# Rotary embedding on one core: empty instruction slots ahead of VectorE's and GpSimd's work

## The chip, the cores and the metric

One Trainium2 chip, of which the kernel uses one core. The metric is the device time of one execution in microseconds (us), as the median of several runs. The engines are named as in the profile: PE (TensorE matmul), PEld (its weight loads), DVE (VectorE), ACT (ScalarE), POOL (GpSimd) and SP (SyncE, which here only issues transfers). "SPq" and "ACTq" are the sequencers of SP and ACT, which start DMAs. The core has 16 DMA engines. q1 is the queue of the transfers that SP starts, q10 that of ACT, and q14, labelled "instruction" in the profile, carries program code.

## The reference

```python
# x (8, 2048, 8, 64) f32; cos, sin (2048, 32) f32
x1 = x[..., :32]
x2 = x[..., 32:]
out1 = x1 * cos - x2 * sin      # cos, sin broadcast over batch and heads
out2 = x1 * sin + x2 * cos
return concatenate([out1, out2], axis=-1)
```

The input and the output have 33.55 MB each, so the core has to move 67 MB and do about three elementwise operations on every element.

## The kernel before

Each of the 8 batch entries `b` is one tile `xt` of 128 partitions by 8192 float32 (4 MB). Five such tiles exist (`NBUF = 5`), and the result is written over the input, in place, before it is stored. SP loads the first five entries at once (`load`, L67), the first of them in pieces of 1, 1 and 2 MB with the `cos` table between; ACT's queue loads the `sin` table (L76). After each of the first three entries has been stored, the load of entry `b + 5` is issued into the buffer that came free.

An entry is worked on in units of 2048 elements for each partition (`UNIT`), or 1024 at the very beginning and end. `rotate` does one unit in one of three ways. Kind A, nearly all of them: POOL writes `t2` with two multiplications (L122, by `sin_sb` and by `nsin`, the negated table), DVE multiplies by the cosine into `t1` (L129) and adds `t1` and `t2` back into `xt` (L136). Kind B, in three units, leaves the addition to PE, which adds with an identity matrix in PSUM (L143, L144), and ACT copies the sum back (L145). Kind C, in two units, takes POOL's work away as well: DVE does a second multiplication (L148), and PE and ACT the rest (L160 to L165).

Program order is fixed on every engine by `keep`, so no scheduler moves anything. Ahead of the loop stand POOL's memset and select that build the identity `eye` (L80, L81), ACT's negated tables and DVE's copy of the cosine table into PSUM (L93). The stores of entries 0 to 6 go out on ACT's queue (L74), those of the last entry, in pieces of 2, 1 and 1 MB, on SP's queue (L74). At the end SP waits for every store (L219).

DVE's whole program is about 110 instructions, the waits on semaphores included, and POOL's about 95.

Of the kernel before, what the change touches and what calls it, by code (L numbers as in the profile page):

```python
# [10 lines left out]
def kernel(  # L11
# [7 lines left out]
    nc = tc.nc  # L19
    keep = tc.keep_in_program_order  # L20
# [43 lines left out]
    def load(b):  # L64
        xt = xpool.tile([P, ROW], f32, tag="xt", name=f"xt{b}")
        for lo, n in spans([UNIT, UNIT, 2 * UNIT] if b == 0 else [ROW]):
            keep(nc.sync.dma_start(out=xt[:, lo : lo + n], in_=xv[b, :, lo : lo + n]))  # L67
            if b == 0 and lo == 0:
                keep(nc.sync.dma_start(out=cos_sb, in_=cos_src))
        xts[b] = xt  # L70
# [6 lines left out]
    for b in range(NBUF):  # L77
        load(b)

    keep(nc.gpsimd.memset(eye, 0.0))  # L80
    nc.gpsimd.affine_select(  # L81
        out=eye,
# [141 lines left out]
```

## Time and profile before

| what | value |
|---|---|
| median of 3 runs | 163.35 us (163.29 to 163.39) |
| profiled execution, its own time | 163.35 us |
| its span, first to last instruction | 161.5 us |
| DVE busy | 140.1 us (87%) |
| POOL busy | 138.9 us (86%) |
| PE busy; ACT busy | 49.2 us; 12.8 us |
| moved by DMA over the span | 67.65 MB, mean 419 GB/s |
| share of the 16 DMA engines, q1 and q10 | 55.3% and 42.8% |

The profiled execution's own time equals the median; it is 1.85 us more than its span, and that part lies outside the instructions shown. All durations below come from this one execution. Busy time of an engine is not by itself a bound: which wait ends last decides.

### The profile page before, as it was taken

What the parts mean: (1) busy time and instruction counts of PE and PEld (TensorE: products, weight loads), DVE (VectorE), ACT (ScalarE), POOL (GpSimd) and SP (SyncE); (2) the same over time, 40 slices, a digit from 0 to 9 for tenths busy, and PEclk for the clock granted to TensorE, in tenths of its full rate; (3) what the DMA queues carried; (4) which work ended last, traced back from release to release, by engine and by line L of the source; (5) the groups of instructions that cost most, each with busy time, mean ns of one, the idle gap of its engine ahead of it and who ended that gap; (6) DMA issues with size and microseconds to landing.
All of it is one profiled execution on the core that took longest, in us unless ns stands there. A gap on an engine that the chain in (4) does not pass through costs nothing.

```text
span 161.5 us, 460 instructions
## 1 busy us (share of the span) xinstructions
PE 49.2 (30%) x80; PEld 18.5 (11%) x80; DVE 140.1 (87%) x66; ACT 12.8 (8%) x14; POOL 138.9 (86%) x70
## 2 busy tenths in 40 slices
PE   0000000597309770978039723973000000000000
PEld 0000000142004220323023302320000000000000
DVE  0297999999999999999999999999999999999600
ACT  3300000002200220021100220022000000000000
POOL 1399997999999999999994999999999999996000
PEclk9999999999975998589956995599655555555555
DMA  5999998998999999999999999999999999999994
GB/s 153 423 458 418 430 487 381 430 487 381 487 398 446 389 462 389 462 446 389 487 422 389 487 416 389 487 422 398 473 422 406 471 422 406 471 422 406 426 404 209
DMA packets 3458, 67.65 MB, mean 419 GB/s; under 512 B 384, under 2 KB 384, under 8 KB 640
## 3 DMA queue, kind: packets, MB, share of 16 engines
q1 hardware_dynamic: 2016, 38.01, 55.3%
q10 hardware_dynamic: 1440, 29.62, 42.8%
q14 instruction: 2, 0.02, 0.0%
HBM read 34.08 MB, written 33.55 MB: 419 GB/s over the span
## 4 chain that ended last, share of the span: by engine, by line
DVE 75%; POOL 9%; issue 6%; DMA 4%; DVEq 0%
DVE t L129 40%; DVE xt L136 33%; POOL t L122 9%; DMA sin_sb<-in_sin_dram 4%; DVE t L148 3%; DVEq L136 0%
## 5 line engine op out<-in xcount | busy, mean ns | idle before, releaser
L122 POOL TENSOR_TENSOR t<-xt,sin_sb 128x1024 f32<-128x1024 f32 (+1 forms) x32 | 71.2, 2226 | 8.5 <-DMA sin_sb<-in_sin_dram 5.3
L129 DVE TENSOR_TENSOR t<-xt,cos_ps 128x2048 f32<-128x2048 f32 (+1 forms) x34 | 73.4, 2166 | 0.8
L122 POOL TENSOR_TENSOR t<-xt,nsin 128x1024 f32<-128x1024 f32 (+1 forms) x32 | 71.3, 2228 | 0.0
L136 DVE TENSOR_TENSOR xt<-t,t 128x2048 f32<-128x2048 f32 (+1 forms) x29 | 62.2, 2145 | 4.2 <-POOL t L122 1.2
L143 PE MATMUL o<-t,eye 128*128 128x512 f32 x24 | 16.9, 797 | 23.1 <-DVE t L129 19.7
L160 PE MATMUL o<-t,eye 128*128 128x512 f32 x16 | 12.0, 842 | 37.9 <-DVE t L129 35.7
L144 PE MATMUL o<-t,eye 128*128 128x512 f32 x24 | 14.9, 709 | 0.0
L145 ACT COPY xt<-o 128x1024 f32<-128x1024 f32 x6 | 6.1, 1012 | 45.7 <-PE o L144 45.7
L143 PEld LDWEIGHTS o<-t,eye 128*128 128x128 f32 x24 | 5.5, 256 | 32.5 <-issue 26.6
L160 PEld LDWEIGHTS o<-t,eye 128*128 128x128 f32 x16 | 3.7, 256 | 43.4 <-issue 39.5
L165 ACT COPY xt<-o 128x1024 f32<-128x1024 f32 x4 | 4.0, 1012 | 47.8 <-PE o L161 47.8
L93 DVE COPY cos_ps<-cos_sb 128x512 f32<-128x512 f32 x1 | 0.7, 695 | 7.1 <-DMA cos_sb<-in_cos_dram 7.1
L144 PEld LDWEIGHTS o<-t,eye 128*128 128x128 f32 x24 | 5.6, 235 | 8.1 <-issue 8.1
L161 PE MATMUL o<-t,neye 128*128 128x512 f32 x8 | 6.2, 872 | 0.2
L148 DVE TENSOR_TENSOR t<-xt,sin_ps 128x2048 f32<-128x2048 f32 x2 | 4.6, 2280 | 0.0
L161 PE MATMUL o<-t,eye 128*128 128x512 f32 x8 | 4.1, 592 | 0.0
L161 PEld LDWEIGHTS o<-t,neye 128*128 128x128 f32 x8 | 2.1, 296 | 5.2 <-issue 3.6
L161 PEld LDWEIGHTS o<-t,eye 128*128 128x128 f32 x8 | 1.5, 190 | 1.9 <-issue 1.9
L90 ACT ACT_TABLE_LOAD x1 | 1.3, 1283 | 1.2 <-PEq L208 1.2
L90 ACT ACTIVATE nsin<-sin_sb 128x512 f32<-128x512 f32 x1 | 0.6, 630 | 4.1 <-DMA sin_sb<-in_sin_dram 4.1
L91 ACT COPY sin_ps<-sin_sb 128x512 f32<-128x512 f32 x1 | 0.6, 578 | 0.0
L80 POOL MEMSET eye<- 128x128 f32 x1 | 0.2, 204 | 0.3 <-POOLq L208 0.3
(6 smaller groups left out, 1.0 us busy)
## 6 DMA issues: line engine op xcount, KB each, us to landing
xt<-in_x_dram SPq DMA_DIRECT2D x7, 4096.0 KB, 34.5
out_dram<-xt ACTq DMA_DIRECT2D x6, 4096.0 KB, 30.5
xt<-in_x_dram SPq DMA_DIRECT2D x2, 1024.0 KB, 6.8
xt<-in_x_dram SPq DMA_DIRECT2D x1, 2048.0 KB, 12.3
out_dram<-xt ACTq DMA_DIRECT2D x2, 1024.0 KB, 19.3
out_dram<-xt ACTq DMA_DIRECT2D x1, 2048.0 KB, 28.0
out_dram<-xt SPq DMA_DIRECT2D x1, 2048.0 KB, 13.5
out_dram<-xt SPq DMA_DIRECT2D x2, 1024.0 KB, 9.9
```

The source lines that it names most:

```text
L90: keep(nc.scalar.mul(nsin, sin_sb, -1.0))
L93: keep(nc.vector.tensor_copy(cos_ps, cos_sb))
L122: nc.gpsimd.tensor_mul(out=t2u[:, :, u, :].rearrange("p (r h) d -> p r h d", h=H), in0=xu[:, :, 1 - u, :].rearrange("p (r h) d -> p r h d" ...
L129: nc.vector.tensor_mul(out=t1.rearrange("p (r k d) -> p r k d", r=nr, d=Dh), in0=xk, in1=rep(cos_ps[:, r0 : r0 + nr, :], 2 * H),)
L136: keep(nc.vector.tensor_add(out=xt, in0=t1, in1=t2))
L143: nc.tensor.matmul(oc, eye, t1[:, cs], start=True, stop=False)
L144: nc.tensor.matmul(oc, eye, t2[:, cs], start=False, stop=True)
L145: keep(nc.scalar.copy(xt[:, 2 * j * C : 2 * (j + 1) * C], o))
L148: nc.vector.tensor_mul(out=t2.rearrange("p (r k d) -> p r k d", r=nr, d=Dh), in0=xk, in1=rep(sin_ps[:, r0 : r0 + nr, :], 2 * H),)
L160: nc.tensor.matmul(oc, eye, t1u[:, gs, u, :], start=True, stop=False)
L161: nc.tensor.matmul(oc, eye if u else neye, t2u[:, gs, 1 - u, :], start=False, stop=True)
L165: nc.scalar.copy(xu[:, :, u, :], o.rearrange("p (g d) -> p g d", d=Dh))
```

## The change

Two directives are put behind the issue of the first loads and ahead of the first instruction of work on POOL and on DVE. A directive becomes no instruction itself. When the program is loaded, it is replaced by as many empty instructions as are needed for the next instruction of that engine to stand at the wanted place: for DVE at a multiple of 128 instruction slots, for POOL at 120 slots past a multiple of 128. How many these are, depends on how many slots the loaded program has ahead of that point, which the source doesn't tell; at most 127 each. No other instruction is added, removed or moved: on every engine the order of the rest is as before. All lines behind the directives have numbers higher by 2.

```diff
     for b in range(NBUF):
         load(b)
 
+    keep(nc.vector.addr_align(128))
+    keep(nc.gpsimd.addr_align(128, offset=120))
     keep(nc.gpsimd.memset(eye, 0.0))
     nc.gpsimd.affine_select(
```

DVE's next instruction is the copy of the cosine table (L93 before), POOL's the memset of `eye` (L80 before).

## The prediction
> **What bounds the kernel now.** I read the page's busy times first, then the DMA queues, then a table by stretches, and last the records of single DMA packets.
>
> ```profile
> PE 49.2 (30%) x80; PEld 18.5 (11%) x80; DVE 140.1 (87%) x66; ACT 12.8 (8%) x14; POOL 138.9 (86%) x70
> ...
> q1 hardware_dynamic: 2016, 38.01, 55.3%
> q10 hardware_dynamic: 1440, 29.62, 42.8%
> q14 instruction: 2, 0.02, 0.0%
> ```
>
> The two data queues take 55.3 + 42.8 = 98.1% of the 16 DMA engines' span; DVE and POOL are less full. In the table by stretches the last two columns are DMA share and GB/s:
>
> ```profile
> 1.70:3.20 1.50, 0.00 (x0) 0.00 (x0) 0.00 (x0) 0.75 (x1) 0.00 (x0) 1.00 0.94 213
> 3.20:8.00 4.80, 0.00 (x0) 0.00 (x0) 0.91 (x2) 1.35 (x3) 1.35 (x2) 1.00 1.00 406
> 8.00:94.00 86.00, 39.50 (x64) 14.72 (x64) 83.16 (x39) 7.21 (x8) 82.96 (x38) 0.88 1.01 432
> ...
> 118.00:152.00 34.00, 0.00 (x0) 0.00 (x0) 32.80 (x17) 0.00 (x0) 30.02 (x16) 0.50 1.00 431
> 152.00:159.40 7.40, 0.00 (x0) 0.00 (x0) 0.20 (x1) 0.00 (x0) 0.00 (x0) 0.50 1.00 423
> 159.40:160.40 1.00, 0.00 (x0) 0.00 (x0) 0.00 (x0) 0.00 (x0) 0.00 (x0) 0.50 0.12 49
> ```
>
> From 3.2 to 159.4 us the DMA engines are full. Before 3.2 they ramp up, and in the last microsecond only 12% of them work. DVE's last instruction starts at 150.98 and ends at 152.21; the rest is stores, for which SP waits at L219:
>
> ```profile
> SPq L219 <- DMA out_dram<-xt: 7.9, 4, 2.4
> ```
>
> So the end is set by the DMA engine that is through with its share last. Every transfer is split evenly over the 16 engines, and each engine's part of a transfer ends in a 4-byte completion record, whose ends I list. For entry 2's store (issued at 62.66) they lie at 93.98 to 94.30, a spread of 0.32. For the last store 14 lie at 159.42 to 159.74, but one at 160.03 and one at 160.36. Two engines have fallen behind, 0.62 us in all at the end. The packets that start in the last moments show it: 5 packets, of which 3 are completion records and 2 are data.
>
> ```profile
> DMA packets 5, 0.02 MB, mean 24 GB/s; under 512 B 3, under 2 KB 3, under 8 KB 3
> ```
>
> What delayed them is on the third queue. Its two packets in the span, of 8192 bytes and 309 ns each, start at 94.09 and 115.84 us; here are the DMA views of 94.0 to 94.4 and of 115.8 to 116.2 (packets, MB, share):
>
> ```profile
> q14 instruction: 1, 0.01, 4.8%
> q10 hardware_dynamic: 13, 0.00, 1.8%
> ```
> ```profile
> q1 hardware_dynamic: 11, 0.36, 212.0%
> q14 instruction: 1, 0.01, 4.8%
> ```
>
> The 32 KB data packet directly behind the first fetch took 1745 ns and that behind the second 1434, where such packets take 1213 nearly everywhere. Each engine's loss is the fetch and the stretch, less the 3 ns by which packets overlap: 309 + 532 - 3 = 838 ns and 309 + 221 - 3 = 527 ns. The first straggler appears among the completions of the next load (109.45, the others by 108.82), the second after 115.84. No engine idles after 3.1 us, so what an engine loses it never makes up. That is the one thing in this kernel that code placement can touch.
>
> **The change, part by part.**
>
> *Empty instructions on DVE.* At most 127. The trace has none; bounds for one are 21 ns (the length of DVE's semaphore records) and 69 ns (two such in a row, 116.110 to 116.179). DVE is past the opening barrier at 0.69 us, so it is ready at 0.69 to 9.5 us. Its first work waits until 7.06 for the cosine table:
>
> ```profile
> 7.06 0.69 DVE L93 COPY cos_ps<-cos_sb 128x512 f32<-128x512 f32 x1 [7.06 <-DMA cos_sb<-in_cos_dram]
> ```
>
> With a middling 64 at 34 ns (GpSimd's rate between memsets at 0.237, 0.271 and 0.305) the pad ends at 2.9 and costs nothing. The worst end is 2.4 us late.
>
> *Empty instructions on POOL.* By the same count, 0 to 127, at 34 to 79 ns (its two semaphore instructions at 0.533 and 0.612): ready at 0.7 to 10.7, middling 2.9. Its first multiplication waits until 6.64 for the sine table, and `eye` ahead of it needs 0.6 us and is first read at 7.65. Middling cost nothing, worst end 4 us late.
>
> *Who covers a late DVE or POOL.* SP and ACT issue the first loads unpadded. The later loads have over 12 us to spare: the last is issued at 94.80, and its queue is busy with the load before until 108.50. Entry 6's store is issued at 132.78, while entry 5's occupies the queue until 139.97. The last store is issued at 152.23; from issue to first packet the first load took 1.0 us, so its packets could go at 153.2, but the engines are busy with the store before it until 156.97. A shift of all DVE work by up to 3.7 us therefore adds nothing. Without that cover a late DVE would cost what it is late.
>
> *The two fetches.* The packets have 8192 bytes, which over 128 slots is 64 bytes a slot. I take one as DVE's and one as POOL's, requested when each moves into its next block of 128 slots. Both DVE and POOL issue something at 92.6, 1.5 us ahead of the first, and at about 113.8, 2.0 us ahead of the second. DVE has some 112 instructions left at the directive, POOL some 85; placed as the change wants them, each stays within one block behind the crossing. The crossings move to DVE's pad and to POOL's ninth instruction, one of its first multiplications. With 1.5 to 2.0 us of delay DVE's fetch lands at about 4.4 to 5 us, and POOL's at 8 to 10. So the fetches are not saved; they come among the first loads.
>
> What is a fetch worth there? Bounds: nothing, if it falls before about 3.1 us, when 8 KB packets take 450 to 1000 ns instead of 309 and the ramp, not the engine, is the limit; and 838 ns, as at 94 us. In between: the packet's own 309 and a stretch of the next. The stretches of 221 and 532 fell on packets of 32 KB; up to 8 us the packets have 2, 8 or 16 KB. If the stretch goes with size, at 8 KB it is a quarter, 55 to 133 ns. I take 0.36 to 0.44 us of loss per engine, nearest to the packet's own row. The two stragglers without their fetches would be at 160.36 - 0.84 = 159.52 and 160.03 - 0.53 = 159.50, where the crowd is; with the early loss they end at 159.86 to 159.96. The last completion moves from 160.36 to about 159.93, and the time by -0.4: 163.35 - 0.4 = 162.95. The floor is the crowd's own last, 159.74, that is -0.62 or 162.73.
>
> [...]
>
> **The rivals.**
>
> *The loss travels along undiminished.* If a fetch costs its engine 0.5 to 0.84 wherever it comes, the stragglers end as late as now: 163.35, at most ±0.2 with the host's place in the crowd. For: the engines are full from 3.2 us on, and the stretch may belong to the fetch and not to the packet behind. Against: the stretches already differ by 2.4 times.
>
> [...]
>
> *Both fetches on one DMA engine.* Now they sit on two. Asked for within a few microseconds of each other, they might be served by one: 0.84 + 0.53 = 1.37 behind the crowd, 159.50 + 1.37 = 160.87, half a microsecond later than now: 163.85. It turns slower once the joint loss passes 0.86. Against: the two stragglers of now. The same sign comes from a pad at its upper end on POOL, 4 us late against 3.7 of cover: +0.3.
>
> **How the numbers follow.** About 0.2%, 0.33 us, is what a measurement of this kernel can tell from no change. Early and cheaper fetches: 0.48, nearly all of it beyond -0.33 (-0.35 to -0.62). Undiminished loss, blocks elsewhere or a loss only a little smaller: 0.38, within ±0.33. One engine for both, or a pad that isn't covered: 0.14. The range reaches from the floor 162.73 (rounded down to 162.7 for the spread of runs, 0.1) to 163.6, which takes in the undiminished case and half of the slower one. The forecast's own range is 162.7 to 163.05.
>
> **What the profile would show.** Right: the two q14 packets start before about 10 us and none later; completions of the last store all within about 0.5 us, the last before 160.0; DVE's copy and POOL's first multiplication still at about 7.0 and 6.6. Wrong: a q14 packet after 20 us; a straggler beyond 160.2 in spite of early fetches; a first copy later than 7.5 with the end later too.

## The result, and the profile after

The changed kernel takes 163.61 us (median of 22 runs, 163.5 to 164.2), the kernel before 163.39 on the same chip (22 runs, 163.26 to 163.78). The ratio is 1.0016, with a 95% interval of 1.0009 to 1.0022: 0.22 us slower, which is inside the 0.2% taken as no change, but not zero by the interval. The forecast was 162.95, its range 162.7 to 163.6. The profiled execution after took 163.58 us with a span of 161.8 (161.775, before 161.548). So 1.80 us lie outside the span in both kernels (the 1.85 given for the kernel before came from its rounded span), and the whole difference, 0.23, is in the span.

Busy times and queues of the page after:

```profile
PE 49.5 (31%) x80; PEld 18.7 (12%) x80; DVE 140.1 (87%) x66; ACT 12.8 (8%) x14; POOL 138.9 (86%) x70
...
q1 hardware_dynamic: 2016, 38.01, 55.4%
q10 hardware_dynamic: 1440, 29.62, 42.6%
q14 instruction: 2, 0.02, 0.0%
```

Work and transfers are the same, down to the packet, and there are still two code packets. The records show the pads themselves: 61 empty instructions on DVE, one every 47 ns from 0.763 to 3.575 us, and 52 on POOL, one every 40 ns from 0.695 to 2.735. The first work behind them, by the timeline after (start, duration, instruction, and in brackets what it waited for):

```profile
6.40 1.27 POOL L124 TENSOR_TENSOR t<-xt,sin_sb 128x512 f32<-128x512 f32 x1 [3.01 <-DMA sin_sb<-in_sin_dram]
6.78 0.69 DVE L95 COPY cos_ps<-cos_sb 128x512 f32<-128x512 f32 x1 [6.78 <-DMA cos_sb<-in_cos_dram]
```

Both still wait for their tables and are 0.24 and 0.28 us earlier than before, so the pads are covered. The table by stretches (DMA share and GB/s in the last two columns) is as full as before:

```profile
1.70:3.20 1.50, 0.00 (x0) 0.00 (x0) 0.00 (x0) 0.75 (x1) 0.31 (x2) 1.00 0.92 225
3.20:8.00 4.80, 0.00 (x0) 0.00 (x0) 1.18 (x2) 1.35 (x3) 1.79 (x3) 1.00 1.04 426
8.00:94.00 86.00, 39.74 (x64) 14.88 (x64) 83.12 (x39) 7.39 (x8) 82.95 (x38) 0.88 1.01 430
...
152.00:159.40 7.40, 0.00 (x0) 0.00 (x0) 0.28 (x1) 0.00 (x0) 0.00 (x0) 0.50 0.99 422
159.40:160.40 1.00, 0.00 (x0) 0.00 (x0) 0.00 (x0) 0.00 (x0) 0.00 (x0) 0.50 0.14 57
```

The code packets have moved. They start at 7.48 and 10.48 us; the DMA views of 7.3 to 7.8 and of 10.3 to 10.8 each hold one (packets, MB, share):

```profile
q1 hardware_dynamic: 26, 0.21, 108.1%
q14 instruction: 1, 0.01, 3.9%
...
q1 hardware_dynamic: 15, 0.25, 118.4%
q14 instruction: 1, 0.01, 3.9%
```

The 8 KB data packet behind the first took 922 ns, 613 more than the 309 of its kind; the 16 KB packet behind the second took 921, 310 more than its kind. With the prediction's formula that is 309 + 613 - 3 = 919 and 309 + 310 - 3 = 616 ns of loss, against 838 and 527 of the late fetches before. Of the last store's 16 completion records 14 end at 159.46 to 159.77 (the crowd), one at 160.14 and one at 160.60 (the stragglers; before, 160.03 and 160.36). SP waits for them as before, and the DMA view of 159.72 to 160.7 shows three completion records and three data packets:

```profile
SPq L221 <- DMA out_dram<-xt: 8.1, 4, 2.4
```
```profile
DMA packets 6, 0.02 MB, mean 25 GB/s; under 512 B 3, under 2 KB 3, under 8 KB 3
```

**Where the 0.23 us come from.** The records do not name the DMA engine. But of the packets behind 3.2 us each starts 3 or 4 ns before the end of another (all 3401 before, 3396 of 3398 after), which is taken as the one ahead of it on its engine. With the transfers of a queue taken in the order of their issue, the engine that ends last can so be followed packet by packet from the end of its part of the cosine table. A packet's duration beyond that of its kind is called a stretch.

| the last DMA engine | before | after | difference |
|---|---|---|---|
| through with the cosine table | 6.555 | 6.258 | -0.30 |
| sum of stretches | 0.80 | 1.33 | +0.53 |
| the fetch itself | 0.306 | 0.306 | 0 |
| last completion | 160.365 | 160.605 | +0.24 |

Before, its stretches were 253 ns at 49.65 us and the 532 behind the fetch. After, they are 613 behind the fetch, 232 at 24.85, 91 at 42.07, and then 113, 109 and 116 at 71.83, 91.30 and 110.78. The other engines have stretches too (a mean of 0.36 us before and 0.66 after, most of it at about 49.5 and 40.5 us), but after 60 us they have 0.02 in the kernel after, where this engine has 0.34. Its three late ones have one place: it alone is still finishing a load on q1 that the others have done, and the packet stretched is q10's first behind that. Net of all this it lags no further: it is 0.95 us behind the median engine at the end of the load behind the fetch (9.64 us) and 0.96 behind at its last completion.

### The profile page after: what moved, and what is told of

The parts are those of the page before. It is cut to its first block, busy times and chain, and to the rows that moved or that the text cites. A ratio compares the mean times of both kernels' runs of the same rounds, so it can differ in the third digit from the quotient of the medians.

```text
span 161.8 us, 573 instructions
## 1 busy us (share of the span) xinstructions
PE 49.5 (31%) x80; PEld 18.7 (12%) x80; DVE 140.1 (87%) x66; ACT 12.8 (8%) x14; POOL 138.9 (86%) x70
## 4 chain that ended last, share of the span: by engine, by line
DMA 46%; DVE 37%; POOL 9%; issue 2%; DVEq 0%; SPq 0%; POOLq 0%; ACTq 0%
DMA xt<-in_x_dram 22%; DMA out_dram<-xt 20%; DVE t L131 18%; DVE xt L138 17%; POOL t L124 9%; DMA sin_sb<-in_sin_dram 3%; DVE t L150 1%; DVEq L138 0%; SPq L67 0%; POOLq L124 0%; ACTq L74 0%
## 5 line engine op out<-in xcount | busy, mean ns | idle before, releaser
L124 POOL TENSOR_TENSOR t<-xt,sin_sb 128x1024 f32<-128x1024 f32 (+1 forms) x32 | 70.4, 2200 | 7.7 <-DMA xt<-in_x_dram 3.3
L124 POOL TENSOR_TENSOR t<-xt,nsin 128x1024 f32<-128x1024 f32 (+1 forms) x32 | 70.4, 2200 | 0.0
L93 ACT COPY sin_ps<-sin_sb 128x512 f32<-128x512 f32 x1 | 0.6, 579 | 0.0
```

The lines of the kernel that those rows point to most:

```text
L124: nc.gpsimd.tensor_mul(out=t2u[:, :, u, :].rearrange("p (r h) d -> p r h d", h=H), in0=xu[:, :, 1 - u, :].rearrange("p (r h) d -> p r h d" ...
```

## The experiments

The times of before differ slightly between chips, so each kernel stands against runs of before on its own chip: 163.37 us for the first four kernels (30 runs), 163.45 for the next three (17), 163.43 for the last two (17). The theories were: a fetch costs its engine 0.5 to 0.9 us whenever it comes, and that decides the end; or the fetch's moment is the price; or something else (the pads, the order of work) is.

**One directive alone.** `e1_dve_only`:

```diff
+    keep(nc.vector.addr_align(128))
```

> Only DVE's directive is kept. Straggler theory: the last DMA engine is the one that carries DVE's code fetch, and GpSimd's fetch sits on another engine that is never last. Then this is as slow as the changed kernel: 163.6, ratio 1.001 to 1.002; one code packet at about 7.5 us with a stretch of some 0.6 us behind it, the other still at about 116 us with 0.2. Rival, the pads or GpSimd's late start cost the time: about half the change, 163.5, or nothing, 163.4, if it is GpSimd's pad alone.

163.71 us (11 runs, 163.5 to 164.55), ratio 1.0023 (1.0013 to 1.0034). Code packets at 7.21 us (+600 ns on the packet behind) and 115.90 (+221). Last completions: 13 at 159.39 to 159.64, then 159.87, 160.08 on the engine of the second fetch and 160.74 on that of the first. The latter has lone stretches of 51, 118 and 138 ns at 71.99, 91.41 and 110.89.

`e2_pool_only`:

```diff
+    keep(nc.gpsimd.addr_align(128, offset=120))
```

> Only GpSimd's directive is kept. Straggler theory: no difference from the kernel before, 163.4, ratio 0.9995 to 1.0005; code packets at about 10.5 us (GpSimd's) and about 94 us (DVE's), the last completion of the last store at 160.3 to 160.4. Rival, GpSimd's pad or its early fetch costs the time: 163.6.

163.45 us (11 runs, 163.32 to 163.84), ratio 1.0007 (0.9999 to 1.0016). Code packets at 10.03 (+331) and 94.08 (+532). The engine of DVE's late fetch ends at 160.355, that of POOL's early one at 160.39, after lone stretches of 203, 120, 148 and 155 ns at 24.65, 71.53, 91.01 and 110.52.

So the packet at 94 us was DVE's and that at 116 POOL's, which the prediction had left open, and each directive moves its own. DVE's accounts for the loss. POOL's early fetch ends where DVE's late one does, and its price is hidden behind that or at the edge of what can be measured.

**A program without a crossing, and the same with an early one.** `e3_short` leaves out the rotation of entries 4 to 7:

```diff
-            rotate(b, lo, n)
+            if b < 4:
+                rotate(b, lo, n)
```

> The kernel before with the rotation of entries 4 to 7 left out (they are loaded and stored as they are), so that DVE's program ends before its crossing at slot 64 of the kernel and GpSimd's before its own. The transfers are the same. Straggler theory: no code packet in the span, all 16 completions of the last store within 0.4 us, and about 0.6 us less than before if the DMA engines stay full: 162.7 to 162.9. Rival, the end is set by something other than the stragglers (arbitration of the two queues, the last store's issue): 163.3 or any other figure, with a spread of the last completions like now.

`e4_short_dvepad` is the same with DVE's directive:

```diff
+    keep(nc.vector.addr_align(128))
...
-            rotate(b, lo, n)
+            if b < 4:
+                rotate(b, lo, n)
```

> The same with the rotation of entries 4 to 7 left out, and DVE's directive added. Straggler theory: one code packet at about 7.5 us, one straggler of some 0.8 to 1.0 us, and the time 0.5 to 0.9 us above the short kernel without the directive. Rival: no more than 0.1 us above it.

Without a crossing: 163.03 us (8 runs, 162.72 to 163.24), ratio 0.9972 (0.9962 to 0.9983). With one at 7.19 us (+603 ns behind it): 163.77 (11 runs, 163.54 to 163.85), 1.0022 (1.0014 to 1.0031). The queues from 0 to 161 us, first without and then with the directive:

```profile
DMA packets 3456, 67.63 MB, mean 420 GB/s; under 512 B 384, under 2 KB 384, under 8 KB 640
q1 hardware_dynamic: 2016, 38.01, 55.6%
q10 hardware_dynamic: 1440, 29.62, 42.8%
```
```profile
DMA packets 3457, 67.64 MB, mean 420 GB/s; under 512 B 384, under 2 KB 384, under 8 KB 640
...
q14 instruction: 1, 0.01, 0.0%
```

The two differ by the pad and one packet of 3457, and by 0.74 us (163.77 - 163.03), or 0.93 us of span in the two profiled executions (161.05 and 161.98 before rounding):

```profile
core 0: 161.0 us, clock 0.707
```
```profile
core 0: 162.0 us, clock 0.701
```

In the first all 16 completions lie within 159.50 and 159.82, and there is no straggler. In the second 15 lie at 159.63 to 159.88 and one at 160.76. This is the price of one fetch by DVE at 7 us, shown without any late fetch beside it. The time falls less than the span: `e3_short` has 1.7 to 2.2 us outside the span where the others have 1.8, and its one code packet at 162.95, behind the span; what that packet does there is open.

**A fetch still earlier, by a jump.** With `max_nops=0` the directive becomes one branch over the slots, in place of empty instructions. `e5_jump`:

```diff
+    keep(nc.vector.addr_align(128, max_nops=0))
+    keep(nc.gpsimd.addr_align(128, offset=120, max_nops=0))
```

> The changed kernel, but both pads are jumped over by one branch (at most one empty instruction runs), so that DVE is in its new block at about 0.8 us instead of 3.6. Theory that a fetch costs its DMA engine 0.9 us anywhere in the full stretch: if DVE's code packet still starts after about 3.2 us, as slow as the changed kernel, 163.5 to 163.7. If it starts before 3.2 us, in the ramp, part of the loss is gone: 162.8 to 163.3, and the last straggler is GpSimd's. Rival, the empty instructions themselves cost the 0.2 us: 163.4, without a change of the last completions.

164.23 us (6 runs, 163.95 to 164.5), ratio 1.0044 (1.003 to 1.0058). The code packets start at 3.76 and 11.06 us. The 8 KB packet behind the first took 840 ns (+531), so nothing is swallowed by the ramp. No empty instruction runs here and the kernel is slower still, which speaks against the empty instructions as the cause. The crowd ends by 159.92 and the straggler at 161.23. Its delay also holds up the cosine table, whose load leaves 16 completion records; by the timeline the copy starts 0.71 us later than before:

```profile
7.77 0.69 DVE L95 COPY cos_ps<-cos_sb 128x512 f32<-128x512 f32 x1 [7.77 <-DMA cos_sb<-in_cos_dram]
```

**Two fetches by one engine.** `e6_twice` sends DVE over one more boundary, ahead of entry 4:

```diff
+    keep(nc.vector.addr_align(128))
...
+        if b == 4:
+            keep(nc.vector.addr_align(128, max_nops=0))
```

> Only DVE's pad at the start, and a second alignment to 128 slots ahead of entry 4's work, jumped over by one branch: DVE crosses a block twice and fetches twice. Theory (one fetch, one loss, always on the same DMA engine): two DVE packets, at about 7.2 us and between 75 and 85 us, the straggler 0.8 to 0.9 us later than with one: last completion at about 161.5, time 164.4 to 164.7. Rival (two fetches on different engines, or losses that don't add): 163.6 to 163.8.

164.6 us (5 runs, 164.5 to 164.95), ratio 1.0067 (1.0054 to 1.008), 0.89 more than with DVE's first directive alone, or 0.81 when each is first set against before on its own chip. There are three code packets, at 7.27 (+606), 83.58 (+535) and 115.93 (+222), and one DMA engine carried the first two:

```profile
q14 instruction: 3, 0.02, 0.0%
```

It ends at 161.97, the next at 160.12. Two fetches by DVE add up on one DMA engine, which loses 309 + 606 - 3 = 912 and 309 + 535 - 3 = 841 ns by them, and the second costs about that much time (0.81 to 0.89 us). One more boundary of 128 slots brought one more packet, of 8192 bytes.

**The moment of DVE's fetch.** `e7_mid` and `e8_late` vary the offset, so that the crossing comes later in DVE's work:

```diff
+    keep(nc.vector.addr_align(128, offset=100))
```

> Only DVE's directive, with an offset of 100 slots: 33 empty instructions, and the crossing at DVE's 29th instruction from there, at about 37 to 42 us. Theory: the loss (0.31 and a stretch of 0.5 to 0.6) is the same here, 163.4 to 163.7, one DVE packet between 38 and 46 us. Rival, the earlier the fetch the dearer, because a straggler loses more later on: between 163.4 and 163.6, below DVE's pad to 128. Rival, half the empty instructions cost half of 0.2 to 0.3 us: 163.5.

```diff
+    keep(nc.vector.addr_align(128, offset=74))
```

> Only DVE's directive, with an offset of 74 slots: 7 empty instructions and the crossing at about 80 us instead of 92. Theory that an early straggler is dearer, because it meets the ends of the transfers (at about 25, 42, 72, 91 and 111 us) alone and its packets are stretched there by 0.1 us or more each: here only one more such end, at 91 us, than before, so 163.4 to 163.6 beside 163.4, below the pads that put the crossing at 3.6 or 42 us. Rival, the empty instructions or any displacement cost the same 0.3 us: 163.7.

`e7_mid`: 163.86 us (11 runs, scattered over 163.47 to 164.51), ratio 1.0027 (1.0014 to 1.004), DVE's packet at 44.64 (+533). `e8_late`: 163.54 (12 runs, 163.28 to 164.01), 1.0004 (0.9989 to 1.0019), packet at 84.43 (+533). In the profile of `e7_mid` DVE's engine ends at 160.56 without a lone stretch after 60 us, but another engine, which carried no fetch, ends at 160.97: it was through with the cosine table only at 7.06 us, where most are at 6.1 to 6.75, and has 1.2 us of stretches. So `e7_mid` is inconclusive on the trend. The five moments, as medians less that of before on the same chip: +0.78 at 3.8 us (`e5_jump`, with POOL's fetch early too), +0.34 at 7.2, +0.41 at 44.6, +0.11 at 84.4, and 0 at 94.1 by definition. The one at 44.6 left aside, a later fetch is cheaper or equal, and no early one gains.

**Less data for the straggler.** `e9_relief` is the kernel before with each table loaded in two pieces, of 104 and 24 partitions, so that some DMA engines carry less. If the one that carries DVE's fetch is among them, the end should come earlier:

```diff
-                keep(nc.sync.dma_start(out=cos_sb, in_=cos_src))
+                for p0, p1 in ((0, 104), (104, P)):
+                    keep(nc.sync.dma_start(out=cos_sb[p0:p1], in_=cos_src[p0:p1]))
...
-    keep(nc.scalar.dma_start(out=sin_sb, in_=sin_src))
+    for p0, p1 in ((0, 104), (104, P)):
+        keep(nc.scalar.dma_start(out=sin_sb[p0:p1], in_=sin_src[p0:p1]))
```

> [...]

164.57 us (6 runs, 164.5 to 164.74), ratio 1.006 (1.0037 to 1.0083). The split changes who carries the tables: each leaves 25 completion records, where it left 16 before. Three engines end early, at 159.13 to 159.52. Ten of the others end at 160.42 to 160.81, about 1 us late, two at 161.18 and 161.23, and the last at 161.64. By an estimate from the trace of before, the extra data explains a third of that 1 us: the tables are 256 packets of 2 KB, 16 for each engine, at 84 ns; if three engines carry none, the other 13 share 48 more, 0.3 us each. More than twenty 8 KB packets at 6.4 to 7.8 us took 220 to 310 ns too long, and DVE began 1.64 us late:

```profile
8.70 0.69 DVE L95 COPY cos_ps<-cos_sb 128x512 f32<-128x512 f32 x1 [8.70 <-DMA cos_sb<-in_cos_dram]
```

DVE's fetch is not carried by one of the three relieved engines, so this relieves the wrong ones. It shows that work moved onto the other engines moves the end, but not what a relief of the right one is worth.

No complete kernel of these is faster than the one before: each moves a fetch or adds one. `e3_short` is faster, but does half the rotation. A program short enough for no crossing with all the work in it was not tried, nor an unequal split of the large transfers.

## Why the prediction was right or wrong

**The bound: right.** The last DMA engine sets the end. DVE's last instruction ended at 152.21 us before and 152.29 after, the span grew by 0.23, and the packet account of the last engine gives +0.24. Where the code packets are taken away (`e3_short`) the straggler goes too. That run takes work off DVE and POOL as well, but `e4_short_dvepad`, with just as little work, is as late as the full kernel.

**The empty instructions: right.** 61 at 47 ns and 52 at 40, against 64 at 34; the pads end at 3.6 and 2.8 us, and the first work stands at 6.78 and 6.40, not later than before.

**The crossings and what moves them: right in kind, late by some.** Both fetches are early and none is late. They came at 7.48 and 10.48, not at 4.4 to 5 and 8 to 10. From crossing to packet it took 3.9 us on DVE, where 1.5 to 2.0 had been read off before. No fixed delay shows: with DVE's records counted as slots, its first instruction behind the boundary starts 0.3 us ahead of the packet in `e7_mid` and 3.5 in `e8_late`.

**The value of an early fetch: the step that failed.** "If the stretch goes with size, at 8 KB it is a quarter, 55 to 133 ns", and so 0.36 to 0.44 us per engine. The stretch behind DVE's fetch was 613 ns on 8 KB (600, 603 and 606 in `e1_dve_only`, `e4_short_dvepad` and `e6_twice`, 531 in `e5_jump`) and 532 to 535 on 32 KB (572 in `e9_relief`); behind POOL's, 310 to 331 on 16 KB and 221 to 235 on 32 KB. It goes with the issuer, or with the DMA engine that carries that issuer's code, which no run separates; and it is no smaller early, on smaller packets. Scaling two readings at one size down to another size had no row behind it: the same two rows, at one size and 2.4 times apart, already said that something other than size sets it. The loss of DVE's engine was 0.92 instead of about 0.4, and the last completion 160.60 instead of 159.93.

**What the sum left out.** The prediction held that an engine's loss is carried to the end unchanged. Of the late fetches that is so: the lag behind the median engine goes from 0.86 to 0.85 us before, and from 0.82 to 0.81 in `e8_late`. Of the early ones it is not in general. After, 0.95 early and 0.96 at the end, two further terms cancel: the last engine has lone stretches of 113, 109 and 116 ns, each where it alone still finishes a load, and against that it misses some of the crowd's. Elsewhere the lag grew, from 0.88 to 1.20 us in `e1_dve_only`, 0.89 to 1.01 in `e4_short_dvepad` and 0.86 to 1.53 in `e5_jump`. Falling behind does not by itself bring the lone stretches. In `e5_jump`, `e6_twice` and `e7_mid` the last engine finishes the same loads (of entries 4 to 6) 1.3 to 2.3 us behind the median, and the packet behind is not stretched. In the kernel after, `e1_dve_only`, `e2_pool_only` and `e4_short_dvepad`, where it is stretched, the engine is 1.6 to 2.3 us behind with its loads but up to 0.7 ahead with its stores; in the three without, it is behind with both. Whether that is the condition was not tested. In the profiled execution, by how far the last engine lies behind the mean of the crowd: 0.825 us before (0.085 at the cosine table, 0.44 of stretches, 0.306 fetch), 0.99 after (0.02, 0.67 and 0.306). Of the 0.67, 0.32 (0.34 - 0.02) came after 60 us. The crowd itself ends 0.07 later (159.54 to 159.61), having begun 0.23 earlier and lost 0.30 more to stretches. 0.99 - 0.825 + 0.07 is the 0.24.

**The rivals.** "The loss travels along undiminished", 163.35 ± 0.2 at 0.38 with its neighbours, is what happened, with 0.24 more at the last completion, which its own ±0.2 did not quite hold. One DMA engine for both did not come about: the two stragglers are two engines after as before, and `e6_twice` shows that it is two fetches of the same issuer that share one. No run shows the "blocks elsewhere" that the 0.38 also counts: one more boundary of 128 slots brought one more packet (`e6_twice`), and one fetch by DVE cost 0.74 us (`e4_short_dvepad` less `e3_short`). On DVE itself the fetch shows no delay: its copy, the first instruction behind its crossing, starts at 6.78 us, before the packet does at 7.48; and in the kernel before the step at 94.91, behind DVE's packet, takes 66 ns as at 90.19.

**A wait that appeared and cost nothing.** The prediction named no new wait on POOL. The straggler's part of entry 7's load lands at 130.26 us, where the others are there by 128.58, and POOL waits for it. By the waits after (us in total, times, longest) and the chain of waits after (start, duration):

```profile
POOL t L124 <- DMA xt<-in_x_dram: 3.3, 2, 2.1
```
```profile
95.09 35.50 DMA xt<-in_x_dram
130.73 4.61 POOL t L124 x2
```

The chain that ended last now runs through that load. DVE's end moved by only 0.08 us, and the last store, issued at 152.31, was behind the store before it in any case, whose completions end at 157.01 to 158.15.

**What stays open.** Why a packet behind a fetch is stretched at all, and DVE's by 531 to 613 ns and POOL's by 221 to 331; why a lone engine's next packet is stretched at the end of a load in four profiles and not in three; what sets the crowd's own stretches at 16 to 24, 40 and 49 us, which differ between executions and may be why runs with mid-program fetches scatter.

## What to carry to other kernels

Where the DMA engines are full from beginning to end, count the code packets too: a crossing that DVE did not feel set the end here, through the one DMA engine that carried the fetch (0.74 us, `e4_short_dvepad` less `e3_short`). Moving a fetch earlier gained nothing here, at 84 us as little as at 7 or 3.8, because the DMA engine lost about as much wherever DVE's fetch came (0.84 to 0.92 us, from 3.8 to 94 us), and a lag from early on grew by the end (by 0.01 to 0.67 us; not from 84 us on). Doing without it is what showed a gain (`e3_short`, with half the rotation); giving its DMA engine less data may pay, which no run here shows. And a cost that was read at one packet size may not be scaled to another by a rule that no second size in the trace supports.

## What the runs showed of the hardware

- A code packet of 8192 bytes took 0.31 us on one DMA engine within the span (before, after), and the data packet behind it was stretched by 0.53 to 0.61 us for DVE's (on packets of 8 and 32 KB) and 0.22 to 0.33 us for POOL's (16 and 32 KB). One fetch by DVE at 7 us made the kernel 0.74 us longer (`e4_short_dvepad` less `e3_short`), and a second one 0.81 to 0.89 more (`e6_twice` against `e1_dve_only`).
- The two fetches of DVE in `e6_twice` went over the same DMA engine, and DVE's and POOL's over two different ones in the profiles of before, after, `e1_dve_only`, `e2_pool_only`, `e6_twice`, `e7_mid` and `e8_late`.
- An empty instruction took 47 ns on DVE (61 of them) and 40 ns on POOL (52; after). In `e5_jump` a branch over the pad took their place, but the fetch came at 3.76 us, where it was dearest (+0.78 us with POOL's).
- A DMA engine that was 0.86 to 0.95 us behind the median after an early fetch was 0.96 to 1.53 behind at the end (after, `e1_dve_only`, `e4_short_dvepad`, `e5_jump`). One put 0.82 to 0.86 behind at 84 or 94 us stayed so. Lone stretches at later loads' ends came in four profiles and not in three others with an engine as far behind.
